# Forget logits as four more columns of each half of the value projection

## The chip, the cores and the metric

The kernel runs on one core of a Trainium2 chip. A core has five engines that run side by side, each through its own list of instructions in a fixed order: TensorE (PE; its loading of stationary operands is shown apart, as PEld), VectorE (DVE), ScalarE (ACT), GpSimd (POOL) and SyncE (SP), which here issues nearly all DMAs, in order, from one queue. The metric is the device time of one execution in microseconds (us); lower is better. A comparison of this kernel can tell about 0.2% from no change.

## The reference

One layer over 2048 positions of width 1024, in float32: two groups of heads (A, B) side by side, then a feed-forward part. What matters here is the input projection and how the forget logits enter attention; the rest is left out.

```python
h = rms_norm(x, norm_mix_g)
z = h @ w_in                      # 1024 -> 512 u | 512 v | 512 q | 512 k | 512 v_b | 8 f
v_b = z[..., 2048:2560].reshape(B, S, 8, 64)
f_logit = z[..., 2560:2568] + f_bias
...
c = cumsum(log_sigmoid(f_logit), axis=1)          # one number per position and head
s = q k^T * scale + c[t] - c[s]                   # causal
out_b = softmax(s) v_b
```

So each of the 8 heads of group B has one logit per position: eight columns of the projection. Attention of a block of queries can begin only when `c` of that block and of the keys before it is there.

## The kernel before

**Precision.** Every float32 matrix product is done as three products of a faster float32 form: an operand is split into a high and a low part (`hi`, `lo`), and `mm3` (L203 to L213) adds hi·hi, hi·lo and lo·hi for each of the 8 blocks of 128 along the contraction: 24 products of 128 by 128 by 512 for one tile of 128 by 512, one PSUM bank. The RMS scale of a row is applied after the product (`self.scales`), since the products take the unscaled, gained x.

**Weights.** `load_unit` (L152) brings 512 KB of weights by DMA into `raw` (2 buffers), lets POOL make `whi` (L150's line in `cast`) and DVE `wlo` (L162); there are 5 buffers of each. A projection to 512 columns needs 4 units, so when one projection follows another, the next one's second to fourth unit wait until the last tile of the one before has used its units.

**Stages.** Phase A takes the positions in two halves of 1024, each in two blocks of 512 (`hT[b]`, features on partitions). `a_half(0)` does keys and queries (features on partitions, `channels`), then values, then `gated` (group A); `a_half(1)` does gated, values, keys and queries. Values and gated are `token_major`: 8 tiles of 128 positions by 512 columns, positions on partitions, in two PSUM banks of tag `mm` that alternate. The end of a values tile: ACT writes the high half from PSUM (L482), DVE the low half (L483), two DMAs take both to DRAM (`vd`).

**Forget logits.** `a_forget(half, b)` (L580) is called four times, between key tiles. It does 16 products with a stationary operand of only 16 columns (`wf`: 8 high, 8 low) and 512 moving columns (L586, L588), so the logits come out with heads on 16 partitions; ACT copies them (L591). `turn`, 12 ticks later, transposes them back with four small products (L596) and takes DVE and ACT through log sigmoid on 128 by 4 by 8 numbers (L599 to L617; Ln needs a table load on ACT). 70 ticks later `cumulate` sums along positions with 8 products against a triangle (L624, L625) and writes `c` split in two to DRAM (`cc` for queries, two rows of `kx` for keys).

**What sets the order.** Each product of `mm3` is a tick. Deferred work (`defer`, `behind`) runs when its tick comes. From the end of `values()` in half 0 on, `fill` steps attention in (`b_stream`): every 3.5 to 4.4 ticks one step, a step being one score tile, first for the maxima (`b_max`: L745, L746, then DVE and ACT) and then for the mix (`b_mix`: L806, L807, exponentials, L794, L795). `need(n)` demands that the fill has finished block n. A scheduler then orders each engine's list by its own estimate of readiness, with weights and fill ahead of the rest (`high_priority`), so attention steps stand earlier than the code has them. After phase A, `c_half` reloads group A's and B's results (`load_mix`) for the output projection; its second block waits until the fill has finished the eighth head of the second 512 queries.

Of the kernel before, what the change touches and what calls it, by code (L numbers as in the profile page):

```python
# [52 lines left out]
def f32(ap):  # L53
    return ap.bitcast(F32)
# [26 lines left out]
class Block:  # L81
# [70 lines left out]
    def load_unit(self, src, inner):  # L152

        nc = self.nc
        raw = self.til(self.rawp, [P, 1024], F32, "raw")
        hi = self.til(self.wpool, [P, 1024], F32R, "whi")
        lo = self.til(self.wpool, [P, 1024], F32R, "wlo")
        v = lambda t: t.rearrange("p (a b) -> p a b", b=inner)
        self.raw_ins = self.dma(raw, src).ins
        with self.tc.high_priority(AHEAD_W):  # L160
            self.cast(hi, raw)
            nc.vector.tensor_tensor(lo, raw, f32(hi), op=ALU.subtract)  # L162
        return v(hi), v(lo)
# [36 lines left out]

        self.split(self.transpose4(pp, tag, cols), g, hi, lo)

    def mm3(self, ps, ah, al, bh, bl):  # L203

        n = len(ah)
        mm = self.nc.tensor.matmul
        for k in range(n):
            mm(ps, lhsT=ah[k], rhs=bh[k], start=k == 0, stop=False)  # L208
            self.tick()
            mm(ps, lhsT=ah[k], rhs=bl[k], start=False, stop=False)  # L210
            self.tick()
            self.last_mm = mm(ps, lhsT=al[k], rhs=bh[k], start=False, stop=k == n - 1).ins  # L212
            self.tick()  # L213


    def constants(self):
# [52 lines left out]
    def a_start(self):  # L269

        nc, sp = self.nc, self.sp
        raws = [self.til(self.rawp, [P, 1024], F32, "raw") for _ in range(2)] + [self.til(sp, [P, 1024], F32, "vn") for _ in range(2)]
        parts = [[self.til(self.wpool, [P, KC, P], F32R, tag) for tag in ("whi", "wlo")] for _ in range(4)]
        v = lambda t: t.rearrange("p (a b) -> p a b", b=P)

        def unit(u, ks):
            raw = v(raws[u])[:, ks, :]
            self.dma(raw, v(self.a["w_in"][4 + u])[:, ks, :])
            hi, lo = [t[:, ks, :] for t in parts[u]]
            self.cast(hi, raw)  # L280
# [18 lines left out]
        self.wf = sp.tile([P, 8, 16], F32R, name="wf")  # L299
        wfr = sp.tile([P, 8, 8], F32, name="wfr")  # L300
        self.dma(wfr, self.a["wf"].rearrange("p (a b) -> p a b", b=8))
        self.fb = sp.tile([P, 8], F32, name="fb")
        self.dma(self.fb, self.a["f_bias"].broadcast_to([P, 8]))
        nc.vector.tensor_copy(self.wf[:, :, 0:8], wfr)
        nc.vector.tensor_tensor(self.wf[:, :, 8:16], wfr, f32(self.wf[:, :, 0:8]), op=ALU.subtract)
# [76 lines left out]
    def a_half(self, half):  # L382
        nc, sp, pp = self.nc, self.sp, self.ap
# [29 lines left out]
        def first_keys():  # L413
# [17 lines left out]
            for u, b in ((2, 0), (3, 0)):  # L431
                for k in range(KC):
                    mms(u, b, k)
            self.a_forget(half, 0)
            for u in range(2):
                for k in range(KC):
                    mms(u, 1, k)
# [7 lines left out]
            self.a_forget(half, 1)  # L445

        def keys_queries():
            if half == 0:
                first_keys()
                groups = (("q", (0, 1)), ("q", (2, 3)))  # L450
            else:
                self.a_scales(1, 0)
                self.a_scales(1, 1)
                u0, u1 = self.a_unit("k", 0), self.a_unit("k", 1)
                self.a_forget(half, 0)
                channels("k", 0, *u0, 0)
                channels("k", 1, *u1, 0)
                self.a_forget(half, 1)
# [12 lines left out]
            if half == 0:  # L471
                with self.tc.issue_after(self.raw_ins):
                    self.a_gate_w(sp, pp)
                    self.scales[1] = [self.a_rows(1, b) for b in range(2)]

        def values():
            for t, ps in token_major(2):
                pv = ps.rearrange("p (h d) -> p h d", h=8)
                hl = self.til(sp, [P, 2, 8, 64], F32R, "vn")
                hi, lo = hl[:, 0, :, :], hl[:, 1, :, :]  # L480
                r = self.scales[half][t // 4][:, t % 4:t % 4 + 1]
                nc.scalar.activation(hi, pv, AF.Copy, scale=r)  # L482
                nc.vector.scalar_tensor_tensor(lo, pv, r, f32(hi), op0=ALU.mult, op1=ALU.subtract)  # L483
                self.dma(self.vd[half][t * P:(t + 1) * P, :, 0:64], f32(hi))
                self.dma(self.vd[half][t * P:(t + 1) * P, :, 64:128], f32(lo))

        def gated():
            vns = []
# [91 lines left out]
    def a_forget(self, half, b):  # L580

        nc, sp, pp = self.nc, self.sp, self.ap
        hT = self.hT[b]
        pl = self.til(pp, [16, TB], F32, "mm" if half else "tp")
        for k in range(KC):
            nc.tensor.matmul(pl, lhsT=self.wf[:, k, :], rhs=hT[0][:, k, :], start=k == 0, stop=False)  # L586
            self.tick()
            nc.tensor.matmul(pl, lhsT=self.wf[:, k, :], rhs=hT[1][:, k, :], start=False, stop=k == KC - 1)  # L588
            self.tick()
        lg = self.til(sp, [16, TB], F32, "ln")  # L590
        nc.scalar.activation(lg, pl, AF.Copy)  # L591

        def turn():
            pt = self.til(pp, [P, 4, 16], F32, "tp")
            for i in range(4):
                nc.tensor.transpose(pt[:, i, :], lg[:, i * P:(i + 1) * P], self.ident[:16, :16])  # L596
            t = lambda: self.til(sp, [P, 4, 8], F32, "fs")
            z0, z = t(), t()
            nc.vector.tensor_copy(z0, pt[:, :, 8:16])  # L599
            nc.vector.tensor_tensor(z, pt[:, :, 0:8], z0, op=ALU.add)  # L600
            nc.vector.tensor_tensor(z, z, self.scales[half][b].unsqueeze(2).broadcast_to([P, 4, 8]), op=ALU.mult)
# [35 lines left out]
        self.defer(12, turn)  # L637

# [837 lines left out]
def _laid_out(a):  # L1476
# [9 lines left out]
    return dict(w_in=c(np.concatenate([tall(w[:, 1024:2048]), wide(w[:, 0:1024]), wide(w[:, 2048:2560])])),  # L1486
                w_out=c(wide(a["w_out"][0])), w_up=c(tall(a["w_up"][0])), xT=c(a["x"][0].T), sgT=c(a["sg_w"][0].transpose(2, 0, 1).reshape(P, 8 * P)),
                wf=c(a["w_in"][0][:, 2560:2568].reshape(KC, P, 8).transpose(1, 0, 2).reshape(P, 64)),
                cols=c(np.concatenate(rows).T))


# [19 lines left out]
```

## Time and profile before

| | |
|---|---|
| time, 3 runs: median (lowest to highest) | 2437.68 us (2436.88 to 2441.38) |
| span of the profiled execution | 2436.2 us |
| mean granted TensorE clock | 0.997 |
| DMA | 400.51 MB in 245031 packets, 164 GB/s over the span |
| phase A (values of half 0 / of half 1) | until about 570 us (108 to 155 / 399 to 459 us) |

The profile gives the span, from the first to the last instruction; no time of that execution besides it is recorded, and the median of the timed runs lies 1.5 us above the span. In the rows quoted below, a row of the timeline has the start in us, the duration in us, engine, line, operation and tiles; a row of groups has the count, then busy time in us and the mean of one in ns; a row of stretches has the stretch, its length, the busy time of each engine with the count of its instructions, the granted clock, the DMA engines' busy share and GB/s. Products on PE are pipelined: one lasts 0.39 us in the rows, while the next starts 0.23 us after it. So the pace is read from starts, not from durations.

### The profile page before, as it was taken

To read this page: it belongs to the slowest core of one execution; us is meant where nothing else is said; L and a number is where in the kernel's file an instruction comes from. 1 tells how busy PE (TensorE), PEld (TensorE's weight loads), DVE (VectorE), ACT (ScalarE), POOL (GpSimd) and SP (SyncE) were. 2 spreads that over 40 slices of the span, in tenths; PEclk is the share of its full clock that TensorE was granted. 3 is DMA by queue.
4 is the path that set the end of the run, shared out by engine and by line. 5 is a ranking of instruction groups with operands and counts; after the bars stand their busy time and mean duration, and the time that the engine had idled before them with its cause. 6 is when DMAs were issued, how large, how long until landed. Compare 5 with 4: busy or idle time off the path is not lost.

```text
span 2436.2 us, 32591 instructions
## 1 busy us (share of the span) xinstructions
PE 2409.5 (99%) x10984; PEld 1982.9 (81%) x10984; DVE 1755.8 (72%) x3086; ACT 1348.5 (55%) x2635; POOL 312.5 (13%) x303
## 2 busy tenths in 40 slices
PE   9999999999999999999999999999999999999998
PEld 7788888788777888888888888888888888888887
DVE  5448776565557878878778774498888877957775
ACT  4347766544455556667676671365555555454443
POOL 3114140000213221111111201100000000000000
PEclk9999999999999999999999999999999999999999
DMA  8854646658756545554555436312222228538633
GB/s 290 276 140 123 199 120 174 169 170 280 215 158 213 187 154 164 163 166 144 179 175 180 157 123 236 140 56 80 85 87 87 78 92 311 164 99 297 206 115 121
DMA packets 245031, 400.51 MB, mean 164 GB/s; under 512 B 51240, under 2 KB 109736, under 8 KB 243440
## 3 DMA queue, kind: packets, MB, share of 16 engines
q1 hardware_dynamic: 239824, 374.31, 48.3%
q0 software_dynamic: 5040, 24.12, 2.5%
q8 instruction: 87, 1.43, 0.2%
q14 instruction: 80, 0.66, 0.1%
HBM read 304.76 MB, written 93.72 MB: 164 GB/s over the span
## 4 chain that ended last, share of the span: by engine, by line
PE 93%; DMA 3%; DVE 1%; ACT 1%; issue 0%; POOL 0%; SPq 0%; DVEq 0%; POOLq 0%; ACTq 0%
PE D L1351 16%; PE mm L210 14%; PE mm L208 14%; PE mm L212 14%; PE A L1149 3%; PE A L1150 3%; PE A L1151 3%; PE o L795 2%; PE o L794 2%; PE s L746 2%; PE s L745 2%; PE s L807 2%; PE s L806 2%; PE B L1150 2%; PE B L1151 2%; PE B L1149 2%
## 5 line engine op out<-in xcount | busy, mean ns | idle before, releaser
L210 PE MATMUL mm<-tlo,whi 128*128 128x512 f32 x912 | 358.1, 393 | 0.0
L208 PE MATMUL mm<-thi,whi 128*128 128x512 f32 x912 | 357.7, 392 | 0.0
L212 PE MATMUL mm<-thi,wlo 128*128 128x512 f32 x912 | 357.5, 392 | 0.0
L208 PE MATMUL mm<-whi,thi 128*128 128x512 f32 x640 | 252.9, 396 | 2.9 <-DMA thi<-mixh 2.2
L150 POOL TENSOR_SCALAR whi<-raw 128x1024 fp32r<-128x1024 f32 (+1 forms) x112 | 125.9, 1125 | 1005.1 <-PE mm L210 616.8
L210 PE MATMUL mm<-wlo,thi 128*128 128x512 f32 x640 | 251.3, 393 | 0.1
L212 PE MATMUL mm<-whi,tlo 128*128 128x512 f32 x640 | 251.0, 393 | 0.0
L754 ACT ACTIVATE s<-s,part 128x512 f32<-128x512 f32 (+3 forms) x261 | 154.6, 592 | 130.7 <-DVE part L749 81.4
L208 PEld LDWEIGHTS mm<-thi,whi 128*128 128x128 f32 x912 | 171.5, 188 | 35.7
L210 PEld LDWEIGHTS mm<-tlo,whi 128*128 128x128 f32 x912 | 171.5, 188 | 35.5
L212 PEld LDWEIGHTS mm<-thi,wlo 128*128 128x128 f32 x912 | 171.5, 188 | 34.8
L818 DVE TENSOR_TENSOR pl<-e,ph 128x512 fp32r<-128x512 f32 (+2 forms) x212 | 136.9, 655 | 76.8 <-ACT ph L817 39.3
L162 DVE TENSOR_TENSOR wlo<-raw,whi 128x1024 fp32r<-128x1024 f32 x104 | 136.2, 1309 | 54.0 <-POOL whi L150 53.6
L812 ACT ACTIVATE e<-s 128x512 f32<-128x512 f32 (+2 forms) x216 | 110.3, 527 | 95.3 <-DVE s L810 41.0
L208 PEld LDWEIGHTS mm<-whi,thi 128*128 128x128 f32 x640 | 120.6, 188 | 26.9 <-DMA thi<-mixh 2.5
L1351 PE MATMUL D<-wl,xh 128*128 128x512 f32 x368 | 141.3, 389 | 0.0
L1351 PE MATMUL D<-wh,xh 128*128 128x512 f32 x368 | 140.8, 389 | 0.2 <-DVE xo L1429 0.2
L212 PEld LDWEIGHTS mm<-whi,tlo 128*128 128x128 f32 x640 | 120.3, 188 | 24.3 <-DMA tlo<-mixl 0.7
L210 PEld LDWEIGHTS mm<-wlo,thi 128*128 128x128 f32 x640 | 120.6, 188 | 23.5 <-DVE wlo L162 0.5
L817 ACT ACTIVATE ph<-e 128x512 fp32r<-128x512 f32 (+2 forms) x212 | 116.3, 562 | 39.5 <-PE o L794 34.1
L1351 PE MATMUL D<-wh,xl 128*128 128x512 f32 x368 | 137.1, 389 | 0.0
L749 DVE TENSOR_REDUCE part<-s 128x1 f32<-128x512 f32 x149 | 98.2, 683 | 21.4 <-PE s L746 20.7
(1898 smaller groups left out, 5853.7 us busy)
## 6 DMA issues: line engine op xcount, KB each, us to landing
raw<-in_w_up_dram SPq DMA_DIRECT2D x72, 512.0 KB
m<-kx SPq DMA_DIRECT2D x133, 256.0 KB
m<-kx SPq DMA_DIRECT2D x160, 136.0 KB
x<-act SPq DMA_DIRECT2D x84, 256.0 KB
raw<-in_w_in_dram SPq DMA_DIRECT2D x36, 512.0 KB
v<-vd SPq DMA_DIRECT2D x66, 256.0 KB
raw<-in_w_out_dram SPq DMA_DIRECT2D x24, 512.0 KB
tw<-in_w_down_dram SPq DMA_DIRECT2D x11, 1024.0 KB
```

Of the source, the lines that this page charges most:

```text
L150: self.cast_ins = self.nc.gpsimd.tensor_scalar(out, in_, 1.0, 0.0, ALU.mult, ALU.add).ins
L162: nc.vector.tensor_tensor(lo, raw, f32(hi), op=ALU.subtract)
L208: mm(ps, lhsT=ah[k], rhs=bh[k], start=k == 0, stop=False)
L210: mm(ps, lhsT=ah[k], rhs=bl[k], start=False, stop=False)
L212: self.last_mm = mm(ps, lhsT=al[k], rhs=bh[k], start=False, stop=k == n - 1).ins
L754: nc.scalar.activation(ps[:, :n], ps[:, :n], AF.Exp, scale=-1.0, bias=dst, accum_out=ls[:, tt, sb:sb + 1])
L817: nc.scalar.activation(ph[:, c], e[:, c], AF.Copy)
L818: nc.vector.tensor_tensor(pl[:, c], e[:, c], f32(ph[:, c]), op=ALU.subtract)
L1149: mm(ps, lhsT=xh[:, ks], rhs=yh[:, k, :], start=fresh and k == 0, stop=False, **kw)
L1150: mm(ps, lhsT=xh[:, ks], rhs=yl[:, k, :], start=False, stop=False, **kw)
L1151: mm(ps, lhsT=xl[:, ks], rhs=yh[:, k, :], start=False, stop=k == 3, **kw)
L1351: nc.tensor.matmul(bank[t], lhsT=x[i][:, ts], rhs=w[k], start=fresh and j == 0 and i + k == 0, stop=last and i == 1, **kw)
```

## The change

The eight forget columns are no longer a projection of their own. `_laid_out` puts four of them behind each 256 value columns (260 + 260 = 520 columns, `w_v`, in units of 128 by 1040), and a tile of 128 positions of the value projection is done as two groups of 128 by 260, each in a PSUM bank of its own. Of each group DVE takes the last four columns, scaled, into `z`, and ACT and DVE split the first 256 as before, in halves. When four tiles are done, log sigmoid starts 3 ticks later from `z`, already with positions on partitions, and `cumulate` 30 ticks after that. The 16-column products, their copy and the transposes back are gone, and so are `wf` and its load. Log sigmoid and `cumulate` themselves are the same. `mm3` counts a tick at every second product in the value projection, so a tile keeps 24 ticks; the 64 ticks of the old products are gone.

```diff
+VW = 260
-        raw = self.til(self.rawp, [P, 1024], F32, "raw")
+        n = src.shape[-1]
+        raw = self.til(self.rawp, [P, n], F32, "raw")
...
-    def mm3(self, ps, ah, al, bh, bl):
+    def mm3(self, ps, ah, al, bh, bl, every=1):
...
+        for i in range(3 * n):
+            k = i // 3
+            a, b = ((ah, bh), (ah, bl), (al, bh))[i % 3]
+            self.last_mm = self.nc.tensor.matmul(ps, lhsT=a[k], rhs=b[k], start=i == 0, stop=i == 3 * n - 1).ins
+            if i % every == 0:
+                self.tick()
...
         def values():
-            for t, ps in token_major(2):
...
+            us = [self.load_unit(self.a["w_v"][j], 2 * VW) for j in range(4)]
+            for t in range(8):
+                b, tsl = t // 4, slice((t % 4) * P, (t % 4 + 1) * P)
+                if t % 4 == 0:
+                    z = self.til(sp, [P, 4, 8], F32, "fs")
                 hl = self.til(sp, [P, 2, 8, 64], F32R, "vn")
...
+                for g in range(2):
+                    ps = self.til(pp, [P, TB], F32, "mm")[:, 0:VW]
+                    cols = slice(g * VW, (g + 1) * VW)
+                    self.mm3(ps, part(b, 0, tsl), part(b, 1, tsl), [us[k // 2][0][:, k % 2, cols] for k in range(KC)],
+                             [us[k // 2][1][:, k % 2, cols] for k in range(KC)], 2)
+                    pv = ps[:, 0:256].rearrange("p (h d) -> p h d", h=4)
...
+                    nc.vector.tensor_scalar(z[:, t % 4, 4 * g:4 * g + 4], ps[:, 256:VW], r, None, ALU.mult)
+                    nc.scalar.activation(hi, pv, AF.Copy, scale=r)
+                    nc.vector.scalar_tensor_tensor(lo, pv, r, f32(hi), op0=ALU.mult, op1=ALU.subtract)
...
+                if t % 4 == 3:
+                    self.defer(3, lambda z=z, b=b: self.a_forget(half, b, z))
...
-        for k in range(KC):
-            nc.tensor.matmul(pl, lhsT=self.wf[:, k, :], rhs=hT[0][:, k, :], start=k == 0, stop=False)
-            self.tick()
-            nc.tensor.matmul(pl, lhsT=self.wf[:, k, :], rhs=hT[1][:, k, :], start=False, stop=k == KC - 1)
-            self.tick()
...
-            self.defer(70, lambda: cumulate(lh, ll))
+            self.defer(30, lambda: cumulate(lh, ll))
```

Line numbers of the changed kernel differ; where rows of it stand below, L211 is its `mm3`, L732 and L733 are L745 and L746, L781 and L782 are L794 and L795, L185 is L183, L611 and L612 are L624 and L625, L164 is L162, L340 is L345 and L391 is L396.

The first place is DVE's list in the start, when the first key tiles wait for the scales of the rows. Before (`rstd` are scales, `wlo` weights, `fs` log sigmoid, `st` a key tile from PSUM):

```order
L363 SCALAR_TENSOR_TENSOR tlo_295<-x_314,cols,thi_293 128x512 x2
L345 TENSOR_SCALAR rstd_320<-ss_321 128x4
L162 TENSOR_TENSOR wlo_776<-raw_774,whi_775 128x1024
L345 TENSOR_SCALAR rstd_340<-ss_341 128x4
L599 COPY fs_543<-tp_538 128x32
L600 TENSOR_TENSOR fs_544<-tp_538,fs_543 128x32
L601 TENSOR_TENSOR fs_544<-fs_544,rstd_320 128x32
L602 TENSOR_TENSOR fs_544<-fs_544,fb 128x32
L396 SCALAR_TENSOR_TENSOR st_590<-mm_405,u_580 128x512
```

And now:

```order
L358 SCALAR_TENSOR_TENSOR tlo_290<-x_309,cols,thi_288 128x512 x2
L340 TENSOR_SCALAR rstd_315<-ss_316 128x4
L164 TENSOR_TENSOR wlo_681<-raw_679,whi_680 128x1024
L164 TENSOR_TENSOR wlo_815<-raw_813,whi_814 128x1024
L340 TENSOR_SCALAR rstd_335<-ss_336 128x4
L391 SCALAR_TENSOR_TENSOR st_536<-mm_400,u_526 128x512
```

The four log-sigmoid instructions are gone from ahead of the first key tile, and the weights of one more unit (`wlo_815`) stand ahead of the second scale instead.

The second place is PE's list in the values of half 0, after the fifth tile (`cumulate` is the products into `tp`; `mm` are value tiles). Now:

```order
L211 MATMUL mm_1307<-wlo_1016,thi_288 128x260
L211 MATMUL mm_1307<-whi_1015,tlo_290 128x260
L611 MATMUL tp_1356<-tri,fr_1281 8x512
L612 MATMUL tp_1356<-tri,fr_1282 8x512
L611 MATMUL tp_1356<-tri,fr_1281 8x384
L612 MATMUL tp_1356<-tri,fr_1282 8x384
L611 MATMUL tp_1356<-tri,fr_1281 8x256
L612 MATMUL tp_1356<-tri,fr_1282 8x256
L611 MATMUL tp_1356<-tri,fr_1281 8x128
L612 MATMUL tp_1356<-tri,fr_1282 8x128
L211 MATMUL mm_1338<-whi_997,thi_287 128x260
```

Before, that stretch of the list held values alone and the first score products of attention, here after the second value tile:

```order
L208 MATMUL mm_1197<-whi_1162,thi_224 128x512
L210 MATMUL mm_1197<-wlo_1163,thi_224 128x512
L212 MATMUL mm_1197<-whi_1162,tlo_226 128x512
L745 MATMUL s_1446<-m_53_394,t_55_396 128x128
L745 MATMUL s_1454<-m_53_394,t_55_396 128x256
L746 MATMUL s_1454<-m_224_1443,t_220_1436 128x256
L208 MATMUL mm_1227<-whi_1144,thi_223 128x512
```

The first score products now stand 72 value products behind `cumulate`, within the seventh of the eight tiles.

The third place is PE's list in the output projection, ahead of its second block (`o` is the mix of the last head that this block needs, `dn` are transposes, `s` scores of later work, `mm` the projection). Before, the mix ends in rows with no projection product among them, and none follows for 24 instructions:

```order
L183 MATMUL dn_6933<-ident,ar_6717 128x128
L795 MATMUL o_6157<-pl_6273,v_6229 128x256
L794 MATMUL o_6157<-ph_6288,v_6229 128x128
L795 MATMUL o_6157<-pl_6289,v_6229 128x128
L745 MATMUL s_6387<-m_52_393,t_54_395 128x512
L746 MATMUL s_6387<-m_1425_6329,t_1422_6323 128x512
L183 MATMUL dn_6982<-ident,ar_6428 128x128
```

Now:

```order
L211 MATMUL mm_7149<-wlo_6704,thi_6684 128x512
L782 MATMUL o_6504<-pl_6620,v_6576 128x256
L781 MATMUL o_6504<-ph_6635,v_6576 128x128
L211 MATMUL mm_7149<-whi_6703,tlo_6686 128x512
L211 MATMUL mm_7149<-whi_6703,thi_6684 128x512
L782 MATMUL o_6504<-pl_6636,v_6576 128x128
L185 MATMUL dn_7177<-ident,ar_6775 128x128
```

The end of the mix has moved in among the projection's products, eight of which, with 12 score products and 20 transposes, stand between it and the first product that needs the reloaded block; before, 16 score products and 8 transposes stood there.

More of the change, by code (lines that the diff above doesn't have):

```diff
@@ L154, in load_unit @@
         nc = self.nc
-        raw = self.til(self.rawp, [P, 1024], F32, "raw")
-        hi = self.til(self.wpool, [P, 1024], F32R, "whi")
-        lo = self.til(self.wpool, [P, 1024], F32R, "wlo")
+        n = src.shape[-1]
+        raw = self.til(self.rawp, [P, n], F32, "raw")
+        hi = self.til(self.wpool, [P, n], F32R, "whi")
+        lo = self.til(self.wpool, [P, n], F32R, "wlo")
         v = lambda t: t.rearrange("p (a b) -> p a b", b=inner)
@@ L201, in transpose_split @@
         self.split(self.transpose4(pp, tag, cols), g, hi, lo)
-    def mm3(self, ps, ah, al, bh, bl):
+    def mm3(self, ps, ah, al, bh, bl, every=1):
         n = len(ah)
-        mm = self.nc.tensor.matmul
-        for k in range(n):
-            mm(ps, lhsT=ah[k], rhs=bh[k], start=k == 0, stop=False)
-            self.tick()
-            mm(ps, lhsT=ah[k], rhs=bl[k], start=False, stop=False)
-            self.tick()
-            self.last_mm = mm(ps, lhsT=al[k], rhs=bh[k], start=False, stop=k == n - 1).ins
-            self.tick()
+        for i in range(3 * n):
[4 more added lines that the diff above has]
+                self.tick()
     def constants(self):
@@ L298, in a_start @@
         self.first = parts
-        self.wf = sp.tile([P, 8, 16], F32R, name="wf")
-        wfr = sp.tile([P, 8, 8], F32, name="wfr")
-        self.dma(wfr, self.a["wf"].rearrange("p (a b) -> p a b", b=8))
         self.fb = sp.tile([P, 8], F32, name="fb")
         self.dma(self.fb, self.a["f_bias"].broadcast_to([P, 8]))
-        nc.vector.tensor_copy(self.wf[:, :, 0:8], wfr)
-        nc.vector.tensor_tensor(self.wf[:, :, 8:16], wfr, f32(self.wf[:, :, 0:8]), op=ALU.subtract)
         self.a_tokens(0, 1, None, 0)
@@ L433, in first_keys @@
                     mms(u, b, k)
-            self.a_forget(half, 0)
             for u in range(2):
@@ L444, in first_keys @@
                 channels("k", u, *self.first[u], 1)
-            self.a_forget(half, 1)
         def keys_queries():
@@ L454, in keys_queries @@
                 u0, u1 = self.a_unit("k", 0), self.a_unit("k", 1)
-                self.a_forget(half, 0)
                 channels("k", 0, *u0, 0)
                 channels("k", 1, *u1, 0)
-                self.a_forget(half, 1)
                 channels("k", 0, *u0, 1)
@@ L476, in values @@
         def values():
-            for t, ps in token_major(2):
-                pv = ps.rearrange("p (h d) -> p h d", h=8)
-                hl = self.til(sp, [P, 2, 8, 64], F32R, "vn")
[L480 to L485, printed above, removed]
+            us = [self.load_unit(self.a["w_v"][j], 2 * VW) for j in range(4)]
[3 more added lines that the diff above has]
+                    z = self.til(sp, [P, 4, 8], F32, "fs")
+                hl = self.til(sp, [P, 2, 8, 64], F32R, "vn")
+                r = self.scales[half][b][:, t % 4:t % 4 + 1]
+                for g in range(2):
[4 more added lines that the diff above has]
+                    pv = ps[:, 0:256].rearrange("p (h d) -> p h d", h=4)
+                    hi, lo = hl[:, 0, 4 * g:4 * g + 4, :], hl[:, 1, 4 * g:4 * g + 4, :]
+                    nc.vector.tensor_scalar(z[:, t % 4, 4 * g:4 * g + 4], ps[:, 256:VW], r, None, ALU.mult)
+                    nc.scalar.activation(hi, pv, AF.Copy, scale=r)
+                    nc.vector.scalar_tensor_tensor(lo, pv, r, f32(hi), op0=ALU.mult, op1=ALU.subtract)
+                self.dma(self.vd[half][t * P:(t + 1) * P, :, 0:64], f32(hl[:, 0, :, :]))
+                self.dma(self.vd[half][t * P:(t + 1) * P, :, 64:128], f32(hl[:, 1, :, :]))
+                if t % 4 == 3:
+                    self.defer(3, lambda z=z, b=b: self.a_forget(half, b, z))
         def gated():
@@ L578, in a_layernorm, with a_forget @@
             self.behind(n, fn)
-    def a_forget(self, half, b):
+    def a_forget(self, half, b, z):
         nc, sp, pp = self.nc, self.sp, self.ap
-        hT = self.hT[b]
-        pl = self.til(pp, [16, TB], F32, "mm" if half else "tp")
-        for k in range(KC):
-            nc.tensor.matmul(pl, lhsT=self.wf[:, k, :], rhs=hT[0][:, k, :], start=k == 0, stop=False)
-            self.tick()
-            nc.tensor.matmul(pl, lhsT=self.wf[:, k, :], rhs=hT[1][:, k, :], start=False, stop=k == KC - 1)
-            self.tick()
-        lg = self.til(sp, [16, TB], F32, "ln")
-        nc.scalar.activation(lg, pl, AF.Copy)
         def turn():
-            pt = self.til(pp, [P, 4, 16], F32, "tp")
-            for i in range(4):
-                nc.tensor.transpose(pt[:, i, :], lg[:, i * P:(i + 1) * P], self.ident[:16, :16])
             t = lambda: self.til(sp, [P, 4, 8], F32, "fs")
[L598 to L601, printed above, removed]
             nc.vector.tensor_tensor(z, z, self.fb.unsqueeze(1).broadcast_to([P, 4, 8]), op=ALU.add)
@@ L635, in cumulate @@
                 self.dma(dst[:, 1, b * TB:(b + 1) * TB], f32(rl))
-        self.defer(12, turn)
+        turn()
     def b_open(self):
@@ L1485, in _laid_out @@
     w = a["w_in"][0]
-    return dict(w_in=c(np.concatenate([tall(w[:, 1024:2048]), wide(w[:, 0:1024]), wide(w[:, 2048:2560])])),
+    wv = np.concatenate([w[:, 2048:2304], w[:, 2560:2564], w[:, 2304:2560], w[:, 2564:2568]], axis=1)
+    return dict(w_in=c(np.concatenate([tall(w[:, 1024:2048]), wide(w[:, 0:1024])])),
+                w_v=c(wv.reshape(4, 2, P, 2 * VW).transpose(0, 2, 1, 3).reshape(4, P, 4 * VW)),
                 w_out=c(wide(a["w_out"][0])), w_up=c(tall(a["w_up"][0])), xT=c(a["x"][0].T), sgT=c(a["sg_w"][0].transpose(2, 0, 1).reshape(P, 8 * P)),
-                wf=c(a["w_in"][0][:, 2560:2568].reshape(KC, P, 8).transpose(1, 0, 2).reshape(P, 64)),
                 cols=c(np.concatenate(rows).T))
```

## The prediction

> **What bounds the kernel now.** The page's busy times come first, then its chain of work that ended last, to see which engine's time counts.
>
> ```profile
> PE 2409.5 (99%) x10984; PEld 1982.9 (81%) x10984; DVE 1755.8 (72%) x3086; ACT 1348.5 (55%) x2635; POOL 312.5 (13%) x303
> PE 93%; DMA 3%; DVE 1%; ACT 1%; issue 0%; POOL 0%; SPq 0%; DVEq 0%; POOLq 0%; ACTq 0%
> ```
>
> PE is busy in 2409.5 of 2436.2 us and 93% of the chain is its own, so PE's list is nearly the time: a product taken out of it pays its pace, if nothing else is late there. A mean over the span doesn't say that it holds in the stretches which the change touches. So the view of stretches comes next: the first forget group, the second half of the key tiles, the values of half 0, those of half 1, and a place far behind, the wait before the output projection's second block.
>
> ```profile
> core 0: us, PE busy (x) PEld busy (x) DVE busy (x) ACT busy (x) POOL busy (x), PEclk, DMA share, GB/s
> 28.70:33.40 4.70, 4.70 (x22) 2.31 (x22) 0.00 (x0) 3.14 (x6) 0.00 (x0) 1.00 1.01 396
> 60.00:80.00 20.00, 20.00 (x94) 14.45 (x93) 10.42 (x26) 7.30 (x12) 1.12 (x2) 1.00 0.86 273
> 108.30:155.10 46.80, 46.80 (x213) 38.83 (x212) 16.59 (x39) 13.22 (x28) 3.17 (x3) 1.00 0.54 148
> 399.20:459.40 60.20, 60.20 (x284) 49.95 (x283) 34.14 (x69) 34.34 (x71) 5.09 (x4) 1.00 0.72 193
> 668.70:681.50 12.80, 7.06 (x28) 4.18 (x26) 9.95 (x19) 9.68 (x25) 0.00 (x0) 0.77 0.50 142
> ```
>
> In the first four PE is busy in every microsecond, at full clock. Only the last has a hole: 5.7 of 12.8 us without a product, at a mean clock of 0.77. In the first the DMA engines are full (1.01), which matters to a rival.
>
> **The change part by part.** (a) *The 64 products with 16 columns go.* One group of 16 runs from the first row here to the second, and 24 products of a values tile from the third to the fourth (starts, from PE's timeline):
>
> ```profile
> 29.64 0.40 PE L586 MATMUL tp<-thi,wf 128*16 128x512 f32 x1
> 33.37 0.40 PE L423 MATMUL s<-thi,whi 128*128 128x512 f32 x1
> 108.34 0.39 PE L208 MATMUL mm<-whi,thi 128*128 128x512 f32 x1
> 113.78 0.39 PE L208 MATMUL mm<-whi,thi 128*128 128x512 f32 x1
> ```
>
> 3.73 us for 16 is 0.233 each: a product with 16 stationary columns cost as much as a whole one (5.44 / 24 = 0.2266). Four groups: **-14.9 us**. Both halves' groups stand among dense products, so all of it is PE's.
>
> (b) *The transposes back go.* The groups view counts them, the timeline shows what one set takes:
>
> ```profile
> L596 PE MATMUL tp<-ident,ln 16*128 16x16 f32 x16 | 1.8, 215 | 0.0
> ...
> 44.06 0.39 PE L425 MATMUL o<-thi,wlo 128*128 128x512 f32 x1
> 44.38 0.42 PE L596 MATMUL tp<-ident,ln 16*128 16x16 f32 x4
> 44.73 0.66 PE L183 MATMUL tp<-ident,st 128*128 128x128 f32 x4
> 46.70 0.66 PE L183 MATMUL tp<-ident,st 128*128 128x128 f32 x4 [1.32 <-ACT st L355]
> 47.12 0.48 PE L208 MATMUL mm<-thi,whi 128*128 128x512 f32 x1
> ```
>
> The next product would have started at 44.06 + 0.23 = 44.29; it starts at 44.73, so 0.44 a set, and four sets are **-1.8**. The copy, the sum and the scaling by DVE and ACT lay beside PE and bring nothing of their own.
>
> (c) *The value products become 768 of 260 columns instead of 384 of 512.* Before they took 16 x 5.44 = 87.0 us. No row has 260 columns. The nearest are score products of 256 and 128 columns, which stand together with their loads:
>
> ```profile
> 934.22 0.28 PE L806 MATMUL dn<-t,m 128*128 128x256 f32 x1
> 934.34 0.28 PE L807 MATMUL dn<-t,m2+_1968_8438 128*128 128x256 f32 x1
> 934.46 0.22 PE L806 MATMUL dn<-t,m 128*128 128x128 f32 x1
> ...
> 934.22 0.19 PEld L807 LDWEIGHTS dn<-t,m2+_1968_8438 128*128 128x128 f32 x1
> 934.34 0.19 PEld L806 LDWEIGHTS dn<-t,m 128*128 128x128 f32 x1
> 934.46 0.19 PEld L807 LDWEIGHTS dn<-t,m2+_1968_8438 128*128 128x128 f32 x1
> 934.57 0.19 PEld L794 LDWEIGHTS o<-ph,v 128*128 128x128 f32 x1
> 934.68 0.19 PEld L210 LDWEIGHTS mm<-tlo,whi 128*128 128x128 f32 x1
> ```
>
> By width alone the pace would be 0.2266 x 260 / 512 = 0.1151, that is 88.4 us or +1.4. The starts of the 256-column products lie 0.12 apart, which at 260 columns is 0.122: 93.7 us or +6.7. The loads, each 0.19 long, start 0.11 to 0.12 apart, so two overlap and the loads have no slack left beside a stream of 0.115. I take 0.118, between the ends, because loads and stream are now equally long and neither hides the other's jitter: 90.6 us, **+3.6** (bounds +1.4 and +6.7). The eight columns themselves cost 768 x 4 columns, that is 1.4 of this; the rest is the smaller product.
>
> (d) *The start.* 4.17 us (16 products and one set of transposes) go ahead of the product at 47.12, which waits for `st`, not for PE: the row at 46.70 shows 1.32 us idle. What sets `st` on DVE:
>
> ```profile
> 40.02 1.23 DVE L162 TENSOR_TENSOR wlo<-raw,whi 128x1024 fp32r<-128x1024 f32 x1 [5.13 <-POOL whi L150]
> 41.16 0.16 DVE L345 TENSOR_SCALAR rstd<-ss 128x4 f32<-128x4 f32 x1
> 46.05 1.29 DVE L396 SCALAR_TENSOR_TENSOR st<-mm,u 128x512 f32<-128x512 f32 x2 [0.34 <-ACT u L357]
> ```
>
> In the new list one more unit's `wlo` stands ahead of this `rstd`. Its buffer is free when the first key tiles are done, 44.06 - 3.73 + 0.39 = 40.7 at the latest. POOL's cast follows (1.05, from the row at 157.78 below), then 1.23 on DVE, 0.16 for `rstd`, half of the 1.29 for the first `st`, and 0.42 for the four transposes (46.70 to 47.12): 44.2. The full saving would put that product at 42.95, so **+1.2** is given back. Bounds: 0 if the buffer comes free sooner, +4.2 if the whole saving becomes waiting.
>
> (e) *Attention's first scores.* They stand 72 value products behind `cumulate`, 72 x 0.118 = 8.5 us, where before the whole values stage lay between. What must fit into that: the sums on DVE and ACT, the writes of `c` by SP's queue and the read back.
>
> ```profile
> 63.33 0.22 PE L625 MATMUL tp<-tri,fr 128*8 128x128 f32 x1
> ...
> 70.34 2.88 SPq L100 DMA_DIRECT2D kx<-vn  x3
> 75.13 0.23 SPq L100 DMA_DIRECT2D t<-cc  x1
> ```
>
> From the last product of `cumulate` to the issue of the first read are 11.8 us, of which 4.8 are SP's own wait for the writes to land; behind that wait stood the weights and tiles that SP was to fetch next. That is 3.3 us over the cover. The DMA engines were at 0.86 there and are at 0.54 in the values, so I take half, **+1.7**; bounds 0 (it fits) and +5 (3.3, and half as much again for the read to land). Late next behind it are the other first scores, which read the same two tensors and wait no further.
>
> *The seam to `gated`.* The units of the values come free in the last group of a tile, which now takes 2.83 us (24 x 0.118) instead of 5.44: the first of them 3/4 of the difference, 2.0 us, later against the end. The last unit of `gated` has no slack to give:
>
> ```profile
> 157.78 1.05 POOL L150 TENSOR_SCALAR whi<-raw 128x1024 fp32r<-128x1024 f32 x1 [4.04 <-PE o L794]
> 158.87 1.23 DVE L162 TENSOR_TENSOR wlo<-raw,whi 128x1024 fp32r<-128x1024 f32 x1 [1.69 <-POOL whi L150]
> 160.59 0.39 PE L210 MATMUL mm<-wlo,thi 128*128 128x512 f32 x1
> ```
>
> `wlo` ends at 160.1 and is read at 160.6. I take **+1.0**: attention's products can stand in for half; bounds 0 and +2.0.
>
> (f) *The wait before the output projection's second block.* The chain from the last head's mix through its division, its write and its reload keeps PE idle:
>
> ```profile
> 668.76 0.27 PE L795 MATMUL o<-pl,v 128*128 128x128 f32 x1
> 681.53 0.79 PE L208 MATMUL mm<-whi,thi 128*128 128x512 f32 x1 [2.22 <-DMA thi<-mixh]
> ```
>
> Now 8 projection products, 12 scores and 20 transposes stand in that hole, before 16 scores and 8 transposes: 8 x 0.2266 + 12 x 0.105 (four transposes took 0.42) - 4 x 0.2266 = 2.2 us more cover. The clock of 0.77 over 12.8 us lost 2.9; with a shorter hole I count some 1.8 of it back. **-4.0**; bounds -9 (all of 5.7 + 2.9 goes) and +3 (the twelve more transposes wait for the chain themselves and stand ahead of the next product, at the low clock).
>
> *At nothing:* the smaller work on DVE (32 takings of four columns) lies beside PE, with DVE at 16.6 of 46.8 us in half 0; without that cover it is the third rival.
>
> Sum: -14.9 - 1.8 + 3.6 + 1.2 + 1.7 + 1.0 - 4.0 = **-13.2**. The profiled execution has a span of 2436.2, the median is 1.5 more; with the same 1.5 the time is 2437.7 - 13.2 = **2424.5**. All bounds at their ends: -24.3 (2413.4) and +4.3 (2442.0).
>
> **The rivals.** *Loads set the pace (slower).* The change doubles the loads, 768 instead of 384 for the values, each 0.19 long. If a load can't overlap its neighbour in a long run, the pace is 0.19: 768 x 0.19 = 145.9, +58.9 in place of +3.6, **2479.8**. It turns the sign from a pace of (87.0 + 16.8) / 768 = 0.135 on. For it: PEld is 38.83 of 46.80 us busy in the values already. Against it: the five loads that start 0.11 to 0.12 apart, though five are few. The Trainium skill, in "TensorE: Matmul & The Clock Gate", section "The mechanism", says that a load of weights overlaps products in flight only where the two use different row groups; by that rule each of these full-height loads would be exposed. This trace disagrees: loads of 0.19 lie behind products whose starts are 0.2266 apart. The same page, section "LDWEIGHTS (loading the stationary operand)", gives columns / 1.2 in ns, 107 for 128 columns, near the 0.11 seen between starts here; by it the loads would just stay under the stream.
>
> *Half 0's saving meets the transfers.* Half 0's share is 32 x 0.233 + 2 x 0.44 = 8.3 us, at the place where DMA stands at 1.01 and 0.86. If the weights and x rows land when they land, PE waits for them instead, and (d) is included: -16.7 + 8.3 + 3.6 + 1.7 + 1.0 - 4.0 = -6.1, **2431.6**. Against it: PE shows no wait for a DMA there before.
>
> *Two banks are too few in half 1.* A group now lasts 2.83 us, and its bank must be empty again one group later. The slowest evicted tile of half 1:
>
> ```profile
> 406.00 0.39 PE L212 MATMUL mm<-whi,tlo 128*128 128x512 f32 x1
> 407.53 0.69 ACT L482 ACTIVATE vn<-mm,rstd 128x512 fp32r<-128x512 f32 x1
> 409.20 0.74 DVE L483 SCALAR_TENSOR_TENSOR vn<-mm,rstd,vn 128x512 fp32r<-128x512 f32 x1
> ```
>
> From the end of its last product (406.39) to DVE's end (409.94) are 3.55 us, 0.72 too long; ACT and DVE are each above 34 of 60 us busy there with attention. At each of 16 groups: +11.5, **2436.0**. Against it: attention's products stand between a group's own and stretch it.
>
> **How the numbers follow.** The forecast has 0.72, the pace of loads 0.08, the transfers 0.10, the two banks 0.10. About 0.2% (4.9 us) is what a measurement of this kernel tells from no change, so faster means below 2432.8 and slower above 2442.6. Faster: 0.68 of the forecast, 0.06 of the transfers, 0.02 of the banks, 0.76. Slower: 0.08 and 0.01 of the banks, 0.09. The rest, 0.15, is the same. The range goes from the lower bound, 2413, to 2437, over both smaller rivals; it leaves out the first rival, some of the banks' and the uppermost of the forecast's bounds, some 0.15.
>
> **What would show it.** No rows with 16 stationary columns; in the values, starts 0.115 to 0.122 apart (0.19 is the first rival); the first values product near 101 (108.3 - 8.3 + 1.2) instead of 108.3 us, or else idle rows before it with a DMA named; idle time before the first scores and in the first `gated` tile, 1.7 and 1.0; groups of half 1 with no wait for DVE; and a hole before the second output block of some 9 instead of 12.8 us. The prediction is wrong most easily in (f), where a list's order far from the edit decides 4 us.

## The result, and the profile after

| | before | after |
|---|---|---|
| median of 20 runs (lowest to highest) | 2438.51 us (2436.56 to 2442.05) | 2442.28 us (2438.75 to 2446.05) |
| span of the profiled execution | 2436.2 us | 2440.5 us |
| mean granted TensorE clock | 0.997 | 0.997 |

The ratio is 1.0014, with a 95% interval of 1.0007 to 1.0020: slower by some 3.4 us, where 13 us less had been forecast. A ratio of 1 lies outside the interval, though the difference is under the 0.2% named above. The page of the changed kernel, its busy times and its chain:

```profile
PE 2412.3 (99%) x11288; PEld 1998.0 (82%) x11288; DVE 1753.2 (72%) x3120; ACT 1351.8 (55%) x2647; POOL 309.5 (13%) x303
PE 90%; DMA 3%; DVE 2%; ACT 2%; issue 1%; POOL 1%; SPq 0%; POOLq 0%; DVEq 0%; ACTq 0%
```

PE is still 99% busy and is busy for longer, 2412.3 instead of 2409.5 us, although 16.7 us of work have gone from its list. So the time wasn't lost to one long wait of PE. The stretches that answer to those of before (second half of the key tiles, values of half 0, values of half 1, the hole before the second output block), in the same columns:

```profile
60.00:80.00 20.00, 20.00 (x89) 16.24 (x88) 8.53 (x13) 5.65 (x10) 3.22 (x3) 1.00 1.00 341
100.90:147.40 46.50, 46.47 (x380) 45.62 (x379) 18.37 (x57) 13.82 (x30) 1.05 (x1) 1.00 0.48 130
394.00:455.00 61.00, 60.38 (x424) 55.84 (x423) 41.02 (x105) 41.38 (x91) 4.51 (x4) 1.00 0.71 195
659.90:673.60 13.70, 7.76 (x43) 5.73 (x42) 9.14 (x14) 9.03 (x22) 0.00 (x0) 0.91 0.60 187
```

In the values of half 0 PE waits for nothing; in half 1 0.6 of 61 us are idle, 0.5 of them in one wait for the read of `cc`. What PE waited for, over the whole span (total us, times, longest):

```profile
PE mm L211 <- DMA thi<-mixh: 4.6, 1, 4.6
PE mm L211 <- DVE st L391: 2.7, 2, 2.0
PE D L1338 <- DVE xo L1416: 2.4, 3, 2.0
...
PE s L732 <- DMA t<-cc: 0.5, 1, 0.5
...
PE mm L211 <- DVE wlo L164: 0.3, 1, 0.3
```

No new wait here is large enough. One that the kernel before doesn't have lies in the last stage (L1338 here, L1351 before), far behind the edit:

```profile
2070.30 0.47 PE L1338 MATMUL D<-wh,xh 128*128 128x512 f32 x1 [2.04 <-DVE xo L1416]
```

The granted clock falls with it, to 0.98 from 2005 to 2100 us, where before it is 1.00. In these two executions the last stage starts at 2006.0 and 2005.6 us and takes 434.5 and 430.6 to the end, so their difference arises there. Over all kept traces this stage takes 429.5 to 435.9 us for the same number of products, 431.4 in after_aligned below; whether the changed kernel's other executions lose these 3.9 us isn't recorded. What has to be found is why 13 us less didn't show ahead of it.

What did change stands in a place that the edit doesn't touch: dense products with 512 columns of keys and queries, before any value product. From PE's timeline, first of the changed kernel, then of the kernel before (whose run goes on into its first value tiles), the ends of a run of 512-column products with nothing between:

```profile
56.88 0.39 PE L211 MATMUL mm<-tlo,whi 128*128 128x512 f32 x1
100.68 0.40 PE L211 MATMUL mm<-thi,wlo 128*128 128x512 f32 x1
```

```profile
83.33 0.45 PE L210 MATMUL mm<-tlo,whi 128*128 128x512 f32 x1
119.00 0.39 PE L212 MATMUL mm<-whi,tlo 128*128 128x512 f32 x1
```

The first run has 190 products: 43.80 / 190 = 0.2305 us. The second has 157: 35.67 / 157 = 0.2272 (0.2274 for its 109 up to the first value product). The durations in the rows are the same, 0.39; only the distance of the starts shows it. The trace gives the same over the whole first part: up to 1580 us, products of 512 columns and full rows that another product follows within 0.3 us start 229.8 ns apart before (some 5850 of them) and 232.5 ns now (some 5400). That is 5400 x 2.7 ns = 14.6 us, most of the 17 us by which the forecast and the result differ. Behind 1580 us both kernels pace alike, at 226.7 and 226.8.

What in the change could slow products that it doesn't touch? It makes the tiles `raw`, `whi` and `wlo` 1040 columns wide instead of 1024. In the built program the tiles of weights then lie 4160 bytes apart instead of 4096, and the tiles between `raw` and them have moved by 128 bytes. Before, nearly all operands of PE started 32 bytes past a multiple of 256. Now the tokens and attention's tiles start at 160, and the weights at 160, 224, 32 and 96 in turn. Behind 1580 us the two operands of a wide product start at the same remainder in both kernels.

### The profile page after: what moved, and what is told of

Its sections match the earlier page's. It is cut to its first block, busy times and chain, and to the rows that moved or that the text cites. A ratio compares the mean times of both kernels' runs of the same rounds, so it can differ in the third digit from the quotient of the medians.

```text
span 2440.5 us, 33272 instructions
## 1 busy us (share of the span) xinstructions
PE 2412.3 (99%) x11288; PEld 1998.0 (82%) x11288; DVE 1753.2 (72%) x3120; ACT 1351.8 (55%) x2647; POOL 309.5 (13%) x303
## 4 chain that ended last, share of the span: by engine, by line
PE 90%; DMA 3%; DVE 2%; ACT 2%; issue 1%; POOL 1%; SPq 0%; POOLq 0%; DVEq 0%; ACTq 0%
PE mm L211 41%; PE D L1338 16%; PE A L1136 3%; PE A L1138 3%; PE A L1137 3%; PE o L782 3%; PE o L781 3%; PE s L732 2%; PE s L733 2%; PE s L793 2%; PE s L794 2%; PE B L1137 2%; PE B L1138 2%; PE B L1136 2%; DMA x<-act 1%
## 5 line engine op out<-in xcount | busy, mean ns | idle before, releaser
L211 PE MATMUL mm<-thi,whi 128*128 128x512 f32 x912 | 360.9, 396 | 2.7 <-DVE st L391 2.7
L211 PE MATMUL mm<-thi,wlo 128*128 128x512 f32 x912 | 360.6, 395 | 0.0
L211 PE MATMUL mm<-tlo,whi 128*128 128x512 f32 x912 | 359.6, 394 | 0.0
L211 PE MATMUL mm<-whi,thi 128*128 128x512 f32 (+1 forms) x768 | 276.8, 361 | 4.7 <-DMA thi<-mixh 4.6
L211 PE MATMUL mm<-wlo,thi 128*128 128x512 f32 (+1 forms) x768 | 275.6, 359 | 0.3 <-DVE wlo L164 0.3
L211 PE MATMUL mm<-whi,tlo 128*128 128x512 f32 (+1 forms) x768 | 275.3, 359 | 0.0
L151 POOL TENSOR_SCALAR whi<-raw 128x1024 fp32r<-128x1024 f32 (+2 forms) x112 | 121.8, 1088 | 1006.5 <-PE mm L211 794.1
L211 PEld LDWEIGHTS mm<-thi,whi 128*128 128x128 f32 x912 | 171.5, 188 | 39.4 <-DVE st L391 2.2
L211 PEld LDWEIGHTS mm<-tlo,whi 128*128 128x128 f32 x912 | 171.6, 188 | 37.5
L211 PEld LDWEIGHTS mm<-thi,wlo 128*128 128x128 f32 x912 | 171.6, 188 | 37.5
L164 DVE TENSOR_TENSOR wlo<-raw,whi 128x1024 fp32r<-128x1024 f32 (+1 forms) x104 | 136.7, 1316 | 51.0 <-POOL whi L151 47.4
L211 PEld LDWEIGHTS mm<-whi,thi 128*128 128x128 f32 x768 | 144.8, 189 | 25.9 <-DMA thi<-mixh 4.8
L211 PEld LDWEIGHTS mm<-wlo,thi 128*128 128x128 f32 x768 | 144.9, 189 | 21.5 <-DVE wlo L164 0.5
L211 PEld LDWEIGHTS mm<-whi,tlo 128*128 128x128 f32 x768 | 144.7, 188 | 21.6
L1338 PE MATMUL D<-wh,xh 128*128 128x512 f32 x368 | 142.0, 391 | 2.2 <-DVE xo L1416 2.2
L1338 PE MATMUL D<-wl,xh 128*128 128x512 f32 x368 | 142.4, 391 | 0.0
L1338 PE MATMUL D<-wh,xl 128*128 128x512 f32 x368 | 139.3, 391 | 0.0
```

What stands on the lines that cost most here:

```text
L151: self.cast_ins = self.nc.gpsimd.tensor_scalar(out, in_, 1.0, 0.0, ALU.mult, ALU.add).ins
L211: self.last_mm = self.nc.tensor.matmul(ps, lhsT=a[k], rhs=b[k], start=i == 0, stop=i == 3 * n - 1).ins
L1338: nc.tensor.matmul(bank[t], lhsT=x[i][:, ts], rhs=w[k], start=fresh and j == 0 and i + k == 0, stop=last and i == 1, **kw)
```

## The experiments

Each edit below is to the kernel before or to the changed one; ratios are against the kernel before, with the runs of the same chip.

**Is it the place itself?** A tile of padding ahead of all others moves all operands but those of attention's second set of tiles alike and leaves every engine's list as it was (128 bytes; also 64 and 224; the room for 128 and 224 comes from one and two buffers of `fs`):

```diff
-        self.ident = cp.tile([P, P], F32, name="ident")
+        self.pad, self.ident = cp.tile([P, 32], F32, name="pad"), cp.tile([P, P], F32, name="ident")
```

> The kernel before, with 128 bytes of padding ahead of every tile in SBUF, so that the operands of nearly all products start 160 instead of 32 bytes past a multiple of 256; the order of every engine's list is that of before. Theory 1 (the start address of the operands sets the pace; in the changed kernel wider weight tiles moved it): the 512-column products of the first 1580 us go from 229.7 to about 232.5 ns apart, some 5800 of them, +16 us: about 2454, and more if the products behind 1580 us, which start at the same remainder, are sensitive too. Theory 2 (the slower pace of the changed kernel comes with its order or with its doubled loads): 229.7 ns and 2438, as before.

> As before_128 with 224 bytes: every operand starts on a multiple of 256. Theory 1, if 32 bytes past 256 is a lucky place: slower, 231 to 233 ns and 2445 to 2456. Theory 1, if only the line matters: as fast as before or faster, down to 226.7 ns everywhere, 2420. Theory 2: 229.7 ns and 2438.

> As before_128 with 64 bytes (96 past a multiple of 256). Theory 1: about 233 ns, as the few products of before whose moving operand stands at 96 past 256 show (233.5), so 2450 to 2460. Theory 2: 229.7 ns and 2438.

Measured: 2435.32 us, ratio 0.9991 (0.9982 to 1.0001); 2439.47, ratio 1.0001 (0.9991 to 1.0012); and 2437.21 in one run. The run of keys and values of before_224:

```profile
83.16 0.45 PE L210 MATMUL mm<-tlo,whi 128*128 128x512 f32 x1
118.83 0.39 PE L212 MATMUL mm<-whi,tlo 128*128 128x512 f32 x1
```

35.67 us for the same 157 products, exactly as before; before_128 and before_64 take 35.68 and 35.67. Theory 1 in this form is refuted: none of the four places (32, 96, 160 and 0 past a multiple of 256) is better than another.

**Does the old spacing bring the old pace back?** The next run is the changed kernel with its tiles padded, in nearly the same order (PE's list differs at 69 of 11288 places); it leaves out the layer norm's gain:

```diff
-        raw = self.til(self.rawp, [P, n], F32, "raw")
-        hi = self.til(self.wpool, [P, n], F32R, "whi")
-        lo = self.til(self.wpool, [P, n], F32R, "wlo")
+        raw = self.til(self.rawp, [P, 1056], F32, "raw")[:, 0:n]
+        hi = self.til(self.wpool, [P, 1088], F32R, "whi")[:, 0:n]
+        lo = self.til(self.wpool, [P, 1088], F32R, "wlo")[:, 0:n]
...
-                nc.gpsimd.tensor_tensor(vn[:, j, :], v[:, j, :], self.lng, op=ALU.mult)
+                nc.gpsimd.tensor_tensor(vn[:, j, :], v[:, j, :], f32(self.tri), op=ALU.mult)
```

> The changed kernel with weight tiles padded so that the operands of the products start 32 bytes past a multiple of 256 again, as before. To make room the layer norm's gain tile is left out and the cumulation's triangle is multiplied in its place. Theory 1: the 512-column products return from 232.5 to about 229.7 ns and the time to about 2426, near the forecast of 2424.5. Theory 2: 232.5 ns and 2442, as the changed kernel.

Measured: 2425.60 us, ratio 0.9952 (0.9937 to 0.9968), and the products of the keys:

```profile
44.37 0.39 PE L211 MATMUL mm<-tlo,whi 128*128 128x512 f32 x1
98.34 0.39 PE L211 MATMUL mm<-thi,wlo 128*128 128x512 f32 x1
```

238 products in 53.97 us, 0.2268 each. So theory 2 falls as well: the order and the doubled loads are still there, and the pace is back. What remains is theory 1b, that the difference of the remainders counts.

**The spacing alone, and a constant difference.** before_wide has only the wider tiles, and leaves out the gain as after_aligned does; before_w64 and before_w128 compute everything, leave the tiles 4096 bytes apart and move all weights together against the rest (before_w128 with 32 columns of padding and one buffer of `fs` less):

```diff
-        raw = self.til(self.rawp, [P, 1024], F32, "raw")
-        hi = self.til(self.wpool, [P, 1024], F32R, "whi")
-        lo = self.til(self.wpool, [P, 1024], F32R, "wlo")
+        raw = self.til(self.rawp, [P, 1040], F32, "raw")[:, 0:1024]
+        hi = self.til(self.wpool, [P, 1040], F32R, "whi")[:, 0:1024]
+        lo = self.til(self.wpool, [P, 1040], F32R, "wlo")[:, 0:1024]
```

```diff
-        self.wpool = es.enter_context(tc.tile_pool(name="wpool", bufs=1))
+        self.wpool = es.enter_context(tc.tile_pool(name="wpool", bufs=1)); self.wpad = self.wpool.tile([P, 16], F32, name="wpad")
```

> The kernel before, with nothing of the change but the width of the weight tiles (1040 columns, of which 1024 are used), PE's list as before. To make room the layer norm's gain tile is left out and the cumulation's triangle multiplied in its place. Theory 1b (not the place itself but its difference counts: products slow down where their operands and those of their neighbours start at different remainders of 256 bytes, which tiles 4160 bytes apart bring about): 512-column products at 232 to 233 ns instead of 229.7 up to 1580 us, +15 to +18 us: 2452 to 2456. Theory 3 (the slower pace needs the 260-column products or the new order as well): 2438.

> The kernel before with 64 bytes of padding ahead of the weight tiles alone: every product of the projections then has its two operands 64 bytes apart modulo 256, in the same order. Theory 1b: 232 to 236 ns in the projections, about 2450. If only a drift among the tiles counts and not a constant difference: 229.7 ns and 2438.

> As before_w64 with 128 bytes. Theory 1b with 256 as the modulus: 231 to 236 ns, about 2450. With 128 as the modulus: 229.7 ns and 2438.

Measured: before_wide 2452.55 us, ratio 1.0056 (1.0041 to 1.0071); before_w64 2455.34 and before_w128 2455.90, one run each. The run of 157 products in the three, in this order:

```profile
84.13 0.45 PE L210 MATMUL mm<-tlo,whi 128*128 128x512 f32 x1
120.41 0.39 PE L212 MATMUL mm<-whi,tlo 128*128 128x512 f32 x1
```

```profile
84.83 0.45 PE L210 MATMUL mm<-tlo,whi 128*128 128x512 f32 x1
121.32 0.39 PE L212 MATMUL mm<-whi,tlo 128*128 128x512 f32 x1
```

```profile
84.89 0.45 PE L210 MATMUL mm<-tlo,whi 128*128 128x512 f32 x1
121.56 0.39 PE L212 MATMUL mm<-whi,tlo 128*128 128x512 f32 x1
```

36.28, 36.49 and 36.67 us, or 0.2311, 0.2324 and 0.2336 a product, where before takes 0.2272. The width of the weight tiles alone, with no product changed and PE's list the same, costs 13 us. Theory 3 falls. What leaving out the gain does to the time by itself wasn't measured; the two runs that keep it lose 16 and 17 us against 2439.35, so the loss doesn't come from there. A constant difference of 64 or of 128 bytes does it too, so a drift among the tiles isn't needed, and equal remainders of 128 aren't enough. In after_aligned the operands agree modulo 256 but not modulo 512, and that is enough for the pace.

**Versions that compute everything.** The gain's tile must stay, so the room has to come from elsewhere: from a buffer of `st`, or from the cumulation's triangle (128 of 512 columns kept; the ones behind them are one column read repeatedly). Both let the scheduler order other rows.

```diff
-    "x": 4, "st": 4, "ln": 2, "vn": 4, "u": 2, "lns": 9, "fs": 9, "fr": 3,
+    "x": 4, "st": 3, "ln": 2, "vn": 4, "u": 2, "lns": 9, "fs": 9, "fr": 3,
```

> As after_aligned, computing all of the reference: the room comes from one buffer of st less (3 instead of 4), which lets the scheduler order some hundred rows of PE otherwise. Theory 1b: pace 229 to 230.5 ns and 2423 to 2430, the spread being the order's. Theory 3: 232 ns and 2442.

> The changed kernel, computing all of the reference, with weight tiles 4352 bytes apart; the room comes from the triangle of the cumulation, of which 128 columns are kept (24 more small products in all, about +2 us), and from one buffer of lns and two of fs; the scheduler orders some other rows too. Theory 1b: 226.9 ns in the keys and 2425 to 2431, under the kernel before and under the changed one.

Measured: after_aligned_valid 2433.26 us, ratio 0.9979 (0.9969 to 0.9989), after_room 2436.98, ratio 0.9997 (0.9984 to 1.0010). The pace of the first in its keys:

```profile
58.76 0.39 PE L211 MATMUL mm<-tlo,whi 128*128 128x512 f32 x1
101.86 0.39 PE L211 MATMUL mm<-thi,wlo 128*128 128x512 f32 x1
```

190 products in 43.10 us, 0.2268: the pace came as expected, with the gain in place. The times came above what was expected of them by 3 and 6 us; both orders differ from after_aligned's. The traces place a part of it in the start: the first value product comes at 98.6 us in after_aligned, at 102.1 in after_aligned_valid and at 101.0 in after_room, with 2.0, 4.2 and 3.0 us of waits for `st` ahead of it and, in the last two, a granted clock of 0.94 from 30 to 60 us instead of 1.00. That is all that separates the spans of the first two (2425.2 and 2428.4), but less than half of what after_room loses (2431.7); the rest stays open.

**The other tiles.** Attention's second set of buffers, opened after some 760 us, stands at another remainder in both kernels. Padding ahead of it puts it right, with every list unchanged:

```diff
-                self.bx = self.bxs.enter_context(self.tc.tile_pool(name="bxpool", bufs=1, side="right", reuse_waits="tile"))
+                self.bxpad = self.bxs.enter_context(self.tc.tile_pool(name="bxpad", bufs=1, side="right")).tile([P, 16], F32, name="bxpad"); self.bx = self.bxs.enter_context(self.tc.tile_pool(name="bxpool", bufs=1, side="right", reuse_waits="tile"))
```

> The kernel before, with 64 bytes of padding ahead of the second set of attention's tiles (bxpool, opened after about 760 us), which stand at 96 past a multiple of 256 while all other operands stand at 32. Theory 1b: from 760 to 1450 us the 512-column products go from 230.3 to 229 ns and below, some 2700 of them, -2 to -5 us: 2433 to 2436. If an operand's place counted only in the projections: 2438.

> after_aligned_valid with 64 bytes of padding ahead of bxpool, in its order. Theory 1b: 2 to 5 us below the 2433 of after_aligned_valid.

> As after_room, with 192 bytes of padding ahead of bxpool, so that its tiles stand at the remainder of the others, in the order of after_room. Theory 1b: 2 to 5 us below after_room.

Measured: before_plus64 2434.58 us, ratio 0.9983 (0.9973 to 0.9992); after_valid_plus 2431.40, ratio 0.9967 (0.9954 to 0.9980); after_room_plus 2435.79, ratio 0.9989 (0.9980 to 0.9999). The stretch from 760 to 1450 us, first of before, then of before_plus64:

```profile
760.00:1450.00 690.00, 689.05 (x3130) 568.77 (x3130) 544.22 (x1068) 461.56 (x1016) 122.62 (x110) 1.00 0.51 165
```

```profile
760.00:1450.00 690.00, 689.57 (x3146) 571.47 (x3145) 547.78 (x1073) 464.02 (x1020) 121.82 (x110) 1.00 0.51 166
```

In the same 690 us PE gets through 16 products more, 0.5% of them, some 3.5 us; its wide products start 229.5 instead of 230.4 ns apart there. In before_64, where the padding puts all other operands at the 96 of this set, they start 229.6 apart. Of the versions that compute everything, after_valid_plus is the fastest, 7 us below the kernel before. Against after_aligned_valid its gain of 1.9 us, and after_room_plus's of 1.2, lie within what these runs can tell.

## Why the prediction was wrong

The sum of 13.2 us was close for what it counted, and lacked a term. By its own steps:

- **(a), (b), the old products and transposes, -16.7.** Their rows are gone. They weren't measured apart; the total below agrees with this size, within an interval of 3.8 us to either side.
- **(c), the split products, +3.6 (bounds +1.4 and +6.7).** The first tile of the changed kernel:

```profile
100.92 0.28 PE L211 MATMUL mm<-whi,thi 128*128 128x260 f32 x1
103.82 0.28 PE L211 MATMUL mm<-whi,thi 128*128 128x260 f32 x1
```

  24 products in 2.90 us are 0.1208 each; over all tiles 0.1209, or 92.8 us, +5.8. In after_aligned it is 0.1198, 92.0 us, +5.0. The size lay between its bounds, 1.4 above the estimate in after_aligned. Why the starts stay 0.120 apart and not 0.115, as the width alone gives, wasn't tested.
- **(d), the start, +1.2.** DVE took `wlo`, then the scales, then `st`, as the new list had it:

```profile
42.08 1.22 DVE L164 TENSOR_TENSOR wlo<-raw,whi 128x1024 fp32r<-128x1024 f32 x1 [4.38 <-POOL whi L151]
43.22 0.16 DVE L340 TENSOR_SCALAR rstd<-ss 128x4 f32<-128x4 f32 x1
43.29 1.28 DVE L391 SCALAR_TENSOR_TENSOR st<-mm,u 128x512 f32<-128x512 f32 x2
...
44.03 0.50 PE L211 MATMUL mm<-thi,whi 128*128 128x512 f32 x1 [2.01 <-DVE st L391]
```

  The product came at 44.03; 44.2 had been worked out. Right, though a second wait for `st`, 0.7 at 56.57 us, wasn't foreseen; after_aligned doesn't have it. The sign that was named for the start, a first value product near 101, came true at 100.92 by luck: the eight products of each of half 0's two `cumulate`, some 2.3 us, stood ahead of it before and stand behind it now, which the sum for that sign left out, and the slower pace and the second wait made up for it. In after_aligned it comes at 98.6.
- **(e), the first scores, +1.7, and the seam, +1.0.** Neither wait came: the 0.5 for `cc` and the 0.3 for `wlo` in the waits above lie at 419 and 338 us, and in the values of half 0 and the first `gated` tiles PE has no idle row. From the last product of `cumulate` to the issue of the first read are now 4.8 us, where 11.8 had been counted:

```profile
130.96 0.22 PE L612 MATMUL tp<-tri,fr 128*8 128x128 f32 x1
...
135.79 0.22 SPq L101 DMA_DIRECT2D t<-cc  x1
```

  The row of before had also been misread: of the 4.8 us ahead of its read SP spent 1.8 waiting for the writes of `cc`, and 2.88 went to three writes to `kx` with a pause among them.
- **(f), the hole, -4.0.** It got longer, not shorter. These rows are of the changed kernel:

```profile
659.96 0.23 PE L782 MATMUL o<-pl,v 128*128 128x128 f32 x1
673.55 0.79 PE L211 MATMUL mm<-whi,thi 128*128 128x512 f32 x1 [4.60 <-DMA thi<-mixh]
```

  13.6 us instead of 12.8, but with 43 instructions in it instead of 28. Idle time stayed at 5.9 (13.70 - 7.76, before 12.80 - 7.06 = 5.7): the 2.2 us of products more were met by a longer chain. It wasn't lengthened by the transposes, as the upper bound had it, but on the way through memory. First before, then now:

```profile
673.88 0.33 SPq L100 DMA_DIRECT2D mixh<-ph  x1
677.20 0.37 SPq L100 DMA_DIRECT2D thi<-mixh  x1
```

```profile
664.34 0.32 SPq L101 DMA_DIRECT2D mixh<-ph  x1
...
669.83 0.37 SPq L101 DMA_DIRECT2D thi<-mixh  x1
```

  The write of the mix is issued sooner after its last product, 4.4 us instead of 5.1, but the reload 5.5 us behind the write instead of 3.3; SP waits 4.3 of these for the write to land, before 2.9. Why it landed later isn't shown. The clock was held down less, 0.91 instead of 0.77: 1.2 us lost instead of 2.9. Some -1.5 in all (0.2 - 1.7), within its bounds.
- **The rivals.** Loads didn't set the pace: 0.121, not 0.19, while PEld was busy in 45.62 of 46.50 us. The Trainium skill's rule that only loads for other row groups overlap ("TensorE: Matmul & The Clock Gate", section "The mechanism") is not borne out: each load lasts 0.19 here, and the starts stay 0.121 apart. The transfers held up nothing, with the DMA engines at 1.00 from 60 to 80 us, and no group of half 1 waited for a bank.

With the measured sizes the sum is -16.7 + 5.0 + 1.1 + 0 - 1.5 = -12.1. The slower pace's 14.6 on top gives +2.5, within the measured interval of 1.7 to 4.9; and after_aligned, which has all of the change but the spacing and leaves out the gain, gained 11.6 (2437.24 to 2425.60; interval 7.8 to 15.4). **What failed is the step that costed the widening of the weight tiles at nothing, by leaving it out.** The part on the change counted the seam to `gated`, the tiles' releases and the smaller DVE work, but took it that every product outside the values keeps its pace. The runs showed in its place a term of +13 us (before_wide alone), spread over more than 5000 products as some 3 ns each. No rival covered it, and so the range ended 5 us below the result; even all upper bounds together (which add up to +4.2, not +4.3) stay under it. The trace of before held a hint that the prediction didn't use: among its wide products up to 1580 us, some 130 whose two operands stand 64 bytes apart modulo 256 start 232 to 234 ns apart, those whose operands agree 228.1 (counting products with another wide one ahead of them and two behind).

Which pairs of operands count is settled in part, when each row is put beside the addresses in the built program, with the same count. In the keys and queries of the changed kernel ahead of its first value product, the 154 products whose own two operands agree modulo 256 start 228.7 ns apart, and those whose operands differ by 64, 128 and 192 start 230.5, 232.4 and 233.8; in before_wide it is 228.9, 230.4, 232.6 and 233.7. So there a product's own two operands count. They aren't all that counts: in after_aligned these products start 227.0 apart, and up to 1580 us even the agreeing ones of the changed kernel start 230.7 apart, against 228.1 before. Whether that comes from their neighbours in the queue no run here separates.

## What to carry to other kernels

A change of a tile's size moves every tile behind it: where an engine is busy all the time, look at the remainders of its operands' addresses before and after, and try tiles padded so that they stay equal (here modulo 256 bytes). When a time moves without a new wait, compare the pace of identical instructions in a stretch that the change doesn't touch, by starts and not by durations. Moving small columns into a large product did pay once the spacing was kept: 11.6 us in the version that leaves out the gain, and in those that compute everything 5.1 us (after_aligned_valid) and 0.7 (after_room, which can't be told from nothing), with a part of the difference in the start of their other orders.

## What the runs showed of the hardware

Products of 512 columns with 128 x 128 stationary operands, both read from SBUF, start 0.2268 to 0.2272 us apart where the operands of a whole run stand at the same remainder of 256 bytes, whichever of the four tried it is (32, 96, 160 or 0), and 0.2305 to 0.2336 where they don't (64 and 128 bytes apart, or drifting by 64 from tile to tile). Their recorded durations, 0.39 in either case, don't show it. Products of 260 columns with a load each run at 0.120 to 0.121 us, 4 to 5% above 260 / 512 of the pace of the wide ones (0.1151).
